# One passage of a transformer layer reordered: the last column group by token tile, units split by token tile, and a later gate product

## The chip, the cores and the metric

The kernel runs on one core of one Trainium2 chip. The metric is device time in microseconds, the median of three runs. One more execution was recorded by the hardware profiler; all durations, waits and orders in time below are from that one.

## The reference

One layer over 256 tokens of 2048 features, fp32, batch 1:

```python
u = _rms_norm(x, norm_mix_pre)
mix = hybrid_mixer(u, ...)      # proj = u @ w_in; three mixers; m = sum of gate * (y @ w_branch); m @ w_out
x = x + _rms_norm(mix, norm_mix_post)
hdn = jnp.square(jax.nn.relu(_rms_norm(x, norm_mlp_pre) @ w_mlp_up))
x = x + _rms_norm(hdn @ w_mlp_down, norm_mlp_post)
```

The mixers are a stick-breaking attention, a forgetting attention and RWKV-7 time mixing. RWKV's result is normed per head, gets a bonus, and is multiplied by a gate `g = sigmoid(gd) @ g_up`. `w_out` is 2048 x 2048, `w_mlp_up` 2048 x 8192.

## The kernel before, in words

**Number format and weights.** TensorE multiplies in a reduced fp32 format, so each fp32 operand is split in two: a rounded high part and the rest. Weights stream from HBM as tiles of 128 x 1024 (512 KB), `wraw` (L142), three buffers. `wsplit` (L148) makes a *pair* of one: ACT copies it, rounding, into `whi` (L151), DVE subtracts that from it into `wlo` (L152); three buffers of each. `wnext` (L155) hands out pairs and keeps `AHEAD` = 1 split in advance. `side` is a list of further loads, issued one by one behind weight loads.

**Activations.** `split` (L225) does the same to an activation of 256 tokens: high part by ACT (L232 with a scale), the rest by DVE (L233), side by side in one *pack* `pk` of 512 columns. `gemm` (L163) multiplies a weight pair with packs, feature-major: `whi` with all 512 columns (L167), `wlo` with the 256 of the high part (L171). `unit` (L177) or `up` (L1056) do two pairs to one PSUM bank `gps`. `tok` (L186) does it the other way round, token-major: for each of the two token tiles of 128 tokens, packs are stationary and 512 weight columns move. Each pair of weights is used for both token tiles at once (L213), but the last `lag` pairs are held, token tile 0 is done with them first (L197), and then token tile 1.

**Order of work.** PE's order up to the last column group of `w_out` is written by hand: the program issues in the order of the text (`written`, a manual schedule on PE), and small pieces of other work run as threads, generators that are resumed by `tick` (L124) when enough microseconds of matmuls, reckoned at 0.227 us each, have gone by. A thread's `yield 7.5` means: go on 7.5 us later by that clock. The other engines, and PE after `written` is closed, are put in order by a scheduler.

**RWKV's gate.** `gate_norm` (L743) is such a thread, run for each half `hf` of the heads. It norms the result, and for each of four head pairs multiplies by `ri` (DVE, L772), applies gain and bias (ACT, L773), adds the bonus (DVE, L774), loads the next pair's `gup` (two DMAs issued on ACT, L751 and L752), multiplies with PE (L778, L779; the *gate product*, into a PSUM bank `mps`, of which there are four) and multiplies the result in (DVE, L780).

**The passage.** Four column groups g of 512 columns of `m @ w_out` are done by `tok`. Each token tile's group gives a sum of squares (ACT, L968), and times the norm's gain goes to `mg` (DVE, L966). When the last group is there, `rstd_of` makes the factor (two operations of POOL, L938, L939), `add_mixed` (L955) adds factor times `mg` to `x1`, that is x + norm(mix). `turned` (L985) transposes `x1` (PE, L987) into `mps` banks, two k-tiles of both token tiles to a bank, and `split` makes the 16 packs `upk2`. For the last group `written` is closed and `lag` is 4. Then the MLP's units begin, each 16 x 512 columns (L167, L175) and 16 x 256 columns (L171). After a unit, `post` (L1069) squares its relu; for the first eight units it also takes the sum of squares of an eighth of `x1` (L1079). The first of the down-projection's weights go through six buffers of their own, `raw2` (L1043).

## Time and profile before

| | us |
|---|---|
| three runs | 1553.29, 1552.16, 1546.8 |
| median | 1552.16 |
| the profiled execution | 1552.68 |
| its span | 1550.9 |

Mean granted TensorE clock 0.997 of full speed. PE is busy 98% of the span, DVE 75%, ACT 58%, POOL 5%. The kernel reads 279.77 MB from HBM, 182 GB/s over the span.

How to read the rows: matmuls are recorded with start and length, and since they are pipelined the lengths overlap; the pitch is read between starts. A number in brackets is the time for which the engine waited before the instruction, with what released it. PE is matmul, PEld the weight load beside it. In a window's row the last three numbers are the granted clock, the share of DMA time, and GB/s.

### The profile page before, as it was taken

To read this page: it belongs to the slowest core of one execution; us is meant where nothing else is said; L and a number is where in the kernel's file an instruction comes from. 1 tells how busy PE (TensorE), PEld (TensorE's weight loads), DVE (VectorE), ACT (ScalarE), POOL (GpSimd) and SP (SyncE) were. 2 spreads that over 40 slices of the span, in tenths; PEclk is the share of its full clock that TensorE was granted. 3 is DMA by queue.
4 is the path that set the end of the run, shared out by engine and by line. 5 is a ranking of instruction groups with operands and counts; after the bars stand their busy time and mean duration, and the time that the engine had idled before them with its cause. 6 is when DMAs were issued, how large, how long until landed. Compare 5 with 4: busy or idle time off the path is not lost.

```text
span 1550.9 us, 22351 instructions
## 1 busy us (share of the span) xinstructions
PE 1515.4 (98%) x8318; PEld 1263.7 (81%) x8318; DVE 1157.1 (75%) x1554; ACT 891.9 (58%) x1326; POOL 84.0 (5%) x155
## 2 busy tenths in 40 slices
PE   7999999999999999999999999999999999999997
PEld 6888888888777788788886888878888887888885
DVE  6865567798548798457656768779988899788855
ACT  7664566554546544455445666667766676666542
POOL 0021000000000100000000000000000000000000
PEclk9999999999999999999999999999999999999999
DMA  7545455445534445435784557878888888887754
GB/s 258 190 165 173 151 184 171 167 152 190 167 121 146 165 160 192 152 134 180 252 285 135 199 186 207 249 219 246 261 248 253 252 239 228 268 241 225 220 194 136
DMA packets 101053, 308.49 MB, mean 199 GB/s; under 512 B 10065, under 2 KB 12497, under 8 KB 100817
## 3 DMA queue, kind: packets, MB, share of 16 engines
q1 hardware_dynamic: 90624, 278.56, 52.5%
q0 software_dynamic: 6912, 25.17, 8.8%
q10 hardware_dynamic: 3408, 3.34, 0.6%
q8 instruction: 65, 1.06, 0.3%
q14 instruction: 44, 0.35, 0.1%
HBM read 279.77 MB, written 2.10 MB: 182 GB/s over the span
## 4 chain that ended last, share of the span: by engine, by line
PE 28%; issue 12%; DMA 11%; DVE 4%; ACT 1%; POOL 0%; POOLq 0%; DVEq 0%; SPq 0%; ACTq 0%
PE gps L213 12%; DMA raw<-raw 7%; PE gps L167 6%; DMA raw<-in_wst_dram 5%; PE gps L171 3%; PE gps L197 3%; DVE wlo L152 2%; ACT whi L151 1%; PE mps L1149 1%; PE mps L1151 1%; PE mps L1150 1%; PE gps L1151 0%; PE gps L175 0%; PE gps L1149 0%; PE gps L1150 0%
## 5 line engine op out<-in xcount | busy, mean ns | idle before, releaser
L152 DVE TENSOR_TENSOR wlo<-raw,whi 128x1024 fp32r<-128x1024 f32 x590 | 715.9, 1222 | 256.5 <-ACT whi L151 238.2
L151 ACT ACTIVATE whi<-raw 128x1024 fp32r<-128x1024 f32 x590 | 618.8, 1056 | 336.8 <-PE gps L213 137.1
L167 PE MATMUL gps<-pk,whi 128*128 128x512 f32 x1495 | 380.3, 393 | 1.2 <-DVE tmp L1072 1.2
L167 PEld LDWEIGHTS gps<-pk,whi 128*128 128x128 f32 x1495 | 276.8, 188 | 58.7 <-issue 4.2
L213 PE MATMUL gps<-whi,pk 128*128 128x512 f32 x1144 | 291.2, 394 | 0.0
L213 PEld LDWEIGHTS gps<-whi,pk 128*128 128x128 f32 x1144 | 213.6, 188 | 45.7 <-issue 1.0
L171 PEld LDWEIGHTS gps<-pk,wlo 128*128 128x128 f32 x1599 | 218.3, 190 | 16.4 <-issue 1.2
L171 PE MATMUL gps<-pk,wlo 128*128 128x256 f32 x1599 | 224.4, 282 | 0.0
L213 PE MATMUL gps<-wlo,pk 128*128 128x512 f32 x572 | 157.4, 394 | 0.0
L213 PEld LDWEIGHTS gps<-wlo,pk 128*128 128x128 f32 x572 | 106.9, 188 | 23.2 <-issue 0.7
L1149 PE MATMUL mps<-whi,fm 128*128 128x512 f32 x192 | 76.2, 397 | 1.1 <-ACT whi L151 1.0
L1071 ACT ACTIVATE tmp<-gps 128x256 f32<-128x256 f32 x64 | 24.5, 383 | 90.7 <-PE gps L175 90.7
L1151 PE MATMUL mps<-wlo,fm 128*128 128x512 f32 x192 | 75.8, 395 | 0.9 <-DVE wlo L152 0.8
L1150 PE MATMUL mps<-whi,fm 128*128 128x512 f32 x192 | 75.1, 391 | 0.0
L1116 POOL DMA_DIRECT2D raw<-raw x48 | 41.9, 873 | 555.5 <-DVE raw L1113 347.5
L197 PE MATMUL gps<-whi,pk 128*128 128x512 f32 x264 | 72.0, 393 | 0.0
L1151 PE MATMUL gps<-wlo,fm 128*128 128x512 f32 x144 | 57.4, 399 | 2.1 <-DVE wlo L152 1.7
L1113 DVE TENSOR_TENSOR raw<-raw,raw 128x1024 f32<-128x1024 f32 x48 | 58.6, 1222 | 1.0
L1149 PE MATMUL gps<-whi,fm 128*128 128x512 f32 x144 | 56.9, 395 | 1.4 <-ACT whi L151 1.4
L197 PEld LDWEIGHTS gps<-whi,pk 128*128 128x128 f32 x264 | 49.3, 188 | 10.6 <-ACT whi L151 0.2
L1150 PE MATMUL gps<-whi,fm 128*128 128x512 f32 x144 | 56.4, 392 | 0.0
L213 PE MATMUL gps<-whi,fm 128*128 128x512 f32 x208 | 51.4, 389 | 0.0
(312 smaller groups left out, 1530.0 us busy)
## 6 DMA issues: line engine op xcount, KB each, us to landing
raw<-in_wst_dram SPq DMA_DIRECT2D x518, 512.0 KB, 4.3
raw<-raw POOLq DMA_DIRECT2D x48, 512.0 KB, 6.3
x<-in_x_dram SPq DMA_DIRECT2D x8, 256.0 KB, 5.5
...
```

What stands on the lines that cost most here:

```text
L151: A.activation(hi, raw, AF.Copy)
L152: V.tensor_tensor(lo, raw, hi.bitcast(F32), ALU.subtract)
L167: PE.matmul(ps, hi[:, i * 128:i * 128 + 128], pks[i], start=first and i == 0, stop=False)
L171: PE.matmul(ps[:, 0:T], lo[:, i * 128:i * 128 + 128], pks[i][:, 0:T], start=False, stop=False)
L197: PE.matmul(ps[tt], pks[k][:, c:c + 128], w[:, (k - k0) * 512:(k - k0) * 512 + 512], start=k == 0 and part == 0 and w is hl[0], stop=w is ...
L213: PE.matmul(ps[tt], pks[k][:, c:c + 128], w[:, (k - k0) * 512:(k - k0) * 512 + 512], start=k == 0 and part == 0 and w is hl[0], stop=False)
L1071: A.activation(b, ps[0][:, T:2 * T], AF.Copy)
L1113: V.tensor_tensor(R[a], R[a], R[b], ALU.add)
L1116: G.dma_start(out=R[a], in_=R[b], accum_op=ALU.add)
L1149: PE.matmul(Q[f], a, w, start=d == 0 and i == 0, stop=False)
L1150: PE.matmul(Q[f], b, w, start=False, stop=False)
L1151: PE.matmul(Q[f], a, wl, start=False, stop=d == 3 and i == 1)
```

## The change

Line numbers behind the first edit are 5 to 33 higher in the changed kernel; L157 there is L152 here, L218 is L213, L202 is L197, L777 to L785 are L772 to L780.

- **Gate product.** For the first half of the heads, `gate_norm` waits 11.5 in place of 7.5 before its four products and 2.8 in place of 2.0 between them.
- **Pairs.** From the first column group of `w_out` to the end of the passage, up to four pairs are split in advance. Three of four splits go to a pool `pa` with nine more buffers for each of `whi` and `wlo`, twelve in all.
- **Last column group.** `lag` is 8: token tile 0 is done with all eight pairs, then token tile 1. PE's order stays written.
- **Token tile 0.** Its x1 is added as before; a thread `turns0` puts its transposes between token tile 1's matmuls, four k-tiles of one token tile to a bank. Splits are of 128 columns, so there are 32 for 16.
- **Two units by token tile.** `share` does units 0 and 1 for one token tile and some k-tiles. Each k-tile costs a matmul of 2 x 128 columns with `whi` and one of 128 with `wlo`. Unit 0's share of tile 0 comes first, then the first transposes of tile 1, then unit 1's share of tile 0, then both units' share of tile 1 by fours.
- **Later.** x1 of tile 1 is added by eight operations of 256 columns with no transpose between. The eight squares of `x1` write to the unit's PSUM bank. `raw2`, `fm` and `sfm` move to a pool opened after `pa` is closed, so that the first six `raw2` loads are issued after the passage.

```diff
     def wsplit(raw):
-        hi = wpool.tile([128, HALF], F32R, tag="whi", name=nm("whi"), bufs=3)
-        lo = wpool.tile([128, HALF], F32R, tag="wlo", name=nm("wlo"), bufs=3)
+        turn[0] += 1
+        if more and turn[0] % 4:
+            hi, lo = (more[0].tile([128, HALF], F32R, tag=t, name=nm(t), bufs=9) for t in ("whi", "wlo"))
+        else:
+            hi, lo = (wpool.tile([128, HALF], F32R, tag=t, name=nm(t), bufs=3) for t in ("whi", "wlo"))
...
-        while len(wq) < 1 + AHEAD and (order or wpos[0] < wst.shape[0]):
+        while len(wq) < 1 + ahead[0] and (order or wpos[0] < wst.shape[0]):
...
-        yield 7.5
+        yield 7.5 if hf else 11.5
...
-            yield 2.0
+            yield 2.0 if hf else 2.8
...
-        return p2.tile([128, 7, 128], F32R, tag="fm", name=nm("fm"), bufs=16)
+        return p3[0].tile([128, 7, 128], F32R, tag="fm", name=nm("fm"), bufs=16)
...
+    more.append(pa)
+    ahead[0] = 4
...
+    upk2 = [pk() for _ in range(KT)]
+
+    def token_half(t, tt):
+        return t.rearrange("p (a t) -> p a t", a=2)[:, :, 128 * tt:128 * tt + 128]
+
+    def turned(k4, tt):
+
+        tr = mps()
+        for i in range(4):
+            PE.transpose(tr[:, 128 * i:128 * i + 128], x1[tt][:, (k4 + i) * 128:(k4 + i) * 128 + 128], C("ident"))
+        for i in range(4):
+            u = token_half(upk2[k4 + i], tt)
+            src = tr[:, 128 * i:128 * i + 128]
+            A.activation(u[:, 0], src, AF.Copy, scale=P("g3", k4 + i))
+            V.scalar_tensor_tensor(u[:, 1], src, P("g3", k4 + i), u[:, 0].bitcast(F32), ALU.mult, ALU.subtract)
+
+    def turns0():
+        for k4 in range(0, KT, 4):
+            yield 1.0 if k4 else 3.6
+            turned(k4, 0)
...
-        if g == 3:
-            assert not threads
-            written.close()
-        for tt, ps in enumerate(tok(mpk, 4 if g == 3 else 1)):
+        assert g < 3 or not threads
+        for tt, ps in enumerate(tok(mpk, 8 if g == 3 else 1)):
...
+            gained()
             if tt == 0:
-                gained()
                 for c in range(0, D, 512):
                     add_mixed(0, c, 512)
-            else:
-                pend = gained
+                start(turns0())
+
+    begun = []
+
+    def share(j, tt, ks):
+
+        if tt == 0 and ks[0] == 0:
+            begun.append((gps(), [wq.pop(0), wq.pop(0)]))
+        ps, hl = begun[j]
+        for k in ks:
+            hi, lo = (w[:, k % 8 * 128:k % 8 * 128 + 128] for w in hl[k // 8])
+            u = token_half(upk2[k], tt)
+            PE.matmul(token_half(ps, tt), hi, u, start=k == 0 and tt == 0, stop=False)
+            PE.matmul(ps[:, 128 * tt:128 * tt + 128], lo, u[:, 0], start=False, stop=k == KT - 1 and tt == 1)
+
+    assert len(wq) == 4 and not threads
+    for c in range(0, D, 256):
+        add_mixed(1, c, 256)
+    share(0, 0, range(KT))
+    turned(0, 1)
+    share(1, 0, range(0, 8))
+    turned(4, 1)
+    share(1, 0, range(8, KT))
+    for c in range(0, KT, 4):
+        if c < 8:
+            turned(c + 8, 1)
+        for j in range(2):
+            share(j, 1, range(c, c + 4))
+    written.close()
+    more.clear()
+    ahead[0] = AHEAD
+    pas.close()
...
-    for k2 in range(0, KT, 2):
-        while len(trs) < min(k2 // 2 + 4, 8):
-            trs.append(mps())
-            turned(2 * len(trs) - 2, 0)
-        if k2 == 8:
-            pend()
-        add_mixed(1, 128 * k2, 256)
-        turned(k2, 1)
-        for i in range(2):
-            u = pk()
-            split(trs[k2 // 2][:, i * T:i * T + T], u, P("g3", k2 + i))
-            upk2.append(u)
...
-        raw = p2.tile([128, HALF], F32, tag="raw2", name=nm("raw"), bufs=6)
+        raw = p3[0].tile([128, HALF], F32, tag="raw2", name=nm("raw"), bufs=6)
...
-                A.activation(junk(), x1[j % 2][:, 512 * (j // 2):512 * (j // 2) + 512], AF.Square,
+                A.activation(ps[0], x1[j % 2][:, 512 * (j // 2):512 * (j // 2) + 512], AF.Square,
...
+        if q == 0 and j < 2:
+            ps[0] = begun[j][0]
+            return [(None, lambda _: posts.append(post))]
```

On PE, in RWKV's first half, before (`gup` is the gate's weights, `wlo`, `whi` and `pk` are matmuls of `tok`, 566 and 568 the small low-rank products):

```order
L566 MATMUL mps_876_4614<-zx_1551,lor_838_4414 128x256
L568 MATMUL mps_877_4616<-zx_1551,lor_838_4414 128x256
L213 MATMUL gps_853_4484<-wlo_866_4556,pk_45_292 128x512
L778 MATMUL mps_885_4641<-zy_1605,gup_872_4596 128x256
L779 MATMUL mps_885_4641<-zz_879,gup_872_4596 128x256
L213 MATMUL gps_854_4485<-wlo_866_4556,pk_45_292 128x512
L213 MATMUL gps_853_4484<-whi_870_4587,pk_46_293 128x512 x2
L213 MATMUL gps_854_4485<-whi_870_4587,pk_46_293 128x512 x2
L213 MATMUL gps_853_4484<-whi_870_4587,pk_47_294 128x512 x2
L213 MATMUL gps_854_4485<-whi_870_4587,pk_47_294 128x512 x2
L778 MATMUL mps_889_4663<-zy_1605,gup_884_4637 128x256
```

and after, from the end of the second gate product to the third:

```order
L784 MATMUL mps_886_4647<-zz_879,gup_870_4592 128x256
L218 MATMUL gps_853_4484<-wlo_869_4577,pk_47_294 128x512
L218 MATMUL gps_854_4485<-wlo_869_4577,pk_47_294 128x512
L218 MATMUL gps_853_4484<-whi_883_4626,pk_48_295 128x512 x2
L218 MATMUL gps_854_4485<-whi_883_4626,pk_48_295 128x512 x2
L218 MATMUL gps_853_4484<-whi_883_4626,pk_49_296 128x512 x2
L218 MATMUL gps_854_4485<-whi_883_4626,pk_49_296 128x512 x2
L218 MATMUL gps_853_4484<-wlo_884_4627,pk_48_295 128x512
L218 MATMUL gps_854_4485<-wlo_884_4627,pk_48_295 128x512
L218 MATMUL gps_853_4484<-wlo_884_4627,pk_49_296 128x512
L783 MATMUL mps_895_4688<-zy_1605,gup_885_4643 128x256
L784 MATMUL mps_895_4688<-zz_879,gup_885_4643 128x256
```

Before, the third product (`mps_885`) follows the low-rank products by one matmul; after, the low-rank products are ahead of the second, and 13 matmuls stand between the second and the third.

On DVE at the same place, before (`g1` is RWKV's result, `b6` another RWKV operand):

```order
L558 TENSOR_SCALAR b6_837_4413<-b6_837_4413 128x512
L772 TENSOR_TENSOR g1_772_3976<-g1_772_3976,gn_841_4422 128x256
L559 TENSOR_TENSOR b6_837_4413<-b6_837_4413 128x512
L152 TENSOR_TENSOR wlo_871_4588<-raw_869_4585,whi_870_4587 128x1024
L774 TENSOR_TENSOR g1_772_3976<-g1_772_3976,g1_503_2610 128x256
L772 TENSOR_TENSOR g1_773_3977<-g1_773_3977,gn_841_4422 128x256
L780 TENSOR_TENSOR g1_772_3976<-mps_868_4570,g1_772_3976 128x256
```

and after:

```order
L563 TENSOR_SCALAR b6_837_4413<-b6_837_4413 128x512
L157 TENSOR_TENSOR wlo_869_4577<-raw_867_4574,whi_868_4576 128x1024
L564 TENSOR_TENSOR b6_837_4413<-b6_837_4413 128x512
L777 TENSOR_TENSOR g1_772_3976<-g1_772_3976,gn_841_4422 128x256
L157 TENSOR_TENSOR wlo_884_4627<-raw_882_4624,whi_883_4626 128x1024
L779 TENSOR_TENSOR g1_772_3976<-g1_772_3976,g1_503_2610 128x256
L777 TENSOR_TENSOR g1_773_3977<-g1_773_3977,gn_841_4422 128x256
L785 TENSOR_TENSOR g1_772_3976<-mps_871_4596,g1_772_3976 128x256
```

A second weight split, `wlo_884`, now stands between the first L772 (777) and the first product's L780 (785). The second L772 still stands just ahead of that.

On ACT there, before, and then after, up to the last DMA for the third product's weights (the first `gup` in the piece of after):

```order
L751 DMA gup_872_4596<-in_gup_dram 128x128
L752 DMA gup_872_4596<-in_gup_dram 32x128
L151 ACTIVATE whi_887_4648<-raw_886_4646 128x1024
L773 ACTIVATE g1_772_3976<-g1_772_3976,par_74 128x256
L751 DMA gup_884_4637<-in_gup_dram 128x128
L752 DMA gup_884_4637<-in_gup_dram 32x128
L151 ACTIVATE whi_895_4684<-raw_894_4682 128x1024
L773 ACTIVATE g1_773_3977<-g1_773_3977,par_74 128x256
```

```order
L756 DMA gup_885_4643<-in_gup_dram 128x128
L778 ACTIVATE g1_772_3976<-g1_772_3976,par_74 128x256
L580 ACTIVATE lw_877_4609<-mps_874_4603,wah_104 128x256
L581 ACTIVATE tha_879_4611<-mps_875_4605,wah_104 128x256
L582 ACTIVATE lw_877_4609<-lw_877_4609,cst_99 128x256
L778 ACTIVATE g1_773_3977<-g1_773_3977,par_74 128x256
L757 DMA gup_885_4643<-in_gup_dram 32x128
```

Before, both DMAs of a pair of heads stand together; after, the second DMA of `gup_885` is behind the second L773 (778).

In the passage, DVE before, from the addition of token tile 0 (`x1_1333`):

```order
L955 SCALAR_TENSOR_TENSOR x1_1333_7018<-mg_1335_7020,rs_1458_7646,x1_1333_7018 128x512 x4
L955 SCALAR_TENSOR_TENSOR x1_1334_7019<-mg_1336_7021,rs_1460_7680,x1_1334_7019 128x256 x4
L233 SCALAR_TENSOR_TENSOR pk_1465_7699<-mps_1461_7684,par_74,pk_1465_7699 128x256
L966 TENSOR_TENSOR mg_1336_7021<-gps_1432_7523,fm_1332_7017 128x512
L955 SCALAR_TENSOR_TENSOR x1_1334_7019<-mg_1336_7021,rs_1460_7680,x1_1334_7019 128x256
L233 SCALAR_TENSOR_TENSOR pk_1466_7702<-mps_1461_7684,par_74,pk_1466_7702 128x256
L233 SCALAR_TENSOR_TENSOR pk_1468_7711<-mps_1462_7687,par_74,pk_1468_7711 128x256
L955 SCALAR_TENSOR_TENSOR x1_1334_7019<-mg_1336_7021,rs_1460_7680,x1_1334_7019 128x256 x3
L233 SCALAR_TENSOR_TENSOR pk_1469_7714<-mps_1462_7687,par_74,pk_1469_7714 128x256
L233 SCALAR_TENSOR_TENSOR pk_1471_7723<-mps_1463_7690,par_74,pk_1471_7723 128x256
L152 TENSOR_TENSOR wlo_1487_7785<-raw_1485_7782,whi_1486_7784 128x1024
```

and after, from the second bank of token tile 0's splits to the last (`x1_1330` is token tile 1):

```order
L983 SCALAR_TENSOR_TENSOR pk_1346_7034<-mps_1480_7698,par_74,pk_1346_7034 128x128
L983 SCALAR_TENSOR_TENSOR pk_1347_7035<-mps_1481_7717,par_74,pk_1347_7035 128x128
L983 SCALAR_TENSOR_TENSOR pk_1348_7036<-mps_1481_7717,par_74,pk_1348_7036 128x128
L997 TENSOR_TENSOR mg_1332_7017<-gps_1453_7555,g2_1338_7026 128x512
L983 SCALAR_TENSOR_TENSOR pk_1349_7037<-mps_1481_7717,par_74,pk_1349_7037 128x128
L967 SCALAR_TENSOR_TENSOR x1_1330_7015<-mg_1332_7017,rs_1483_7762,x1_1330_7015 128x256 x2
L983 SCALAR_TENSOR_TENSOR pk_1350_7038<-mps_1481_7717,par_74,pk_1350_7038 128x128
L983 SCALAR_TENSOR_TENSOR pk_1351_7039<-mps_1482_7736,par_74,pk_1351_7039 128x128
L967 SCALAR_TENSOR_TENSOR x1_1330_7015<-mg_1332_7017,rs_1483_7762,x1_1330_7015 128x256 x2
L983 SCALAR_TENSOR_TENSOR pk_1352_7040<-mps_1482_7736,par_74,pk_1352_7040 128x128
L967 SCALAR_TENSOR_TENSOR x1_1330_7015<-mg_1332_7017,rs_1483_7762,x1_1330_7015 128x256 x2
L983 SCALAR_TENSOR_TENSOR pk_1353_7041<-mps_1482_7736,par_74,pk_1353_7041 128x128
```

Before, splits are of 256 columns and come after the additions of their columns; after, the additions of tile 1 stand between the last splits of tile 0.

PE in the passage, before, where the transposes turn into matmuls:

```order
L987 MATMUL mps_1461_7684<-ident_73,x1_1334_7019 128x128 x2
L987 MATMUL mps_1462_7687<-ident_73,x1_1334_7019 128x128 x2
L987 MATMUL mps_1463_7690<-ident_73,x1_1334_7019 128x128 x2
L987 MATMUL mps_1464_7693<-ident_73,x1_1334_7019 128x128 x2
L167 MATMUL gps_1488_7788<-pk_1465_7699,whi_1455_7634 128x512
L167 MATMUL gps_1495_7833<-pk_1465_7699,whi_1490_7807 128x512
L987 MATMUL mps_1467_7705<-ident_73,x1_1333_7018 128x128 x2
L987 MATMUL mps_1467_7705<-ident_73,x1_1334_7019 128x128 x2
L167 MATMUL gps_1488_7788<-pk_1466_7702,whi_1455_7634 128x512
```

and after, where unit 0's share of token tile 0 ends:

```order
L1022 MATMUL gps_1484_7774<-pk_1353_7041,whi_1470_7618 128x2x128
L1023 MATMUL gps_1484_7774<-pk_1353_7041,wlo_1471_7619 128x128
L1022 MATMUL gps_1484_7774<-pk_1354_7042,whi_1470_7618 128x2x128
L1023 MATMUL gps_1484_7774<-pk_1354_7042,wlo_1471_7619 128x128
L978 MATMUL mps_1485_7807<-ident_73,x1_1330_7015 128x128 x4
L1022 MATMUL gps_1486_7820<-pk_1339_7027,whi_1473_7630 128x2x128
L1023 MATMUL gps_1486_7820<-pk_1339_7027,wlo_1474_7631 128x128
L1022 MATMUL gps_1486_7820<-pk_1340_7028,whi_1473_7630 128x2x128
L1023 MATMUL gps_1486_7820<-pk_1340_7028,wlo_1474_7631 128x128
```

Before, PE has products of two units for each pack; after, all 32 products of unit 0's share of tile 0 stand ahead of tile 1's first transposes (`mps_1485`), and unit 1's (`gps_1486`) behind them.

27 lines of the change are left out of this document (14 added, 13 removed).

## The prediction

> **What bounds the kernel now.** I read the page first, for the shares.
>
> ```profile
> span 1550.9 us, 22351 instructions
> PE 1515.4 (98%) x8318; PEld 1263.7 (81%) x8318; DVE 1157.1 (75%) x1554; ACT 891.9 (58%) x1326; POOL 84.0 (5%) x155
> ```
>
> PE stands still for 1550.9 - 1515.4 = 35.5 us in all. A change that leaves the number of products alone can win a part of that, and what the clock loses, no more. So I asked next for PE's waits.
>
> ```profile
> PE gps L309 <- ACT whi L151: 8.8, 1, 8.8
> PE mps L987 <- DVE x L955: 2.1, 2, 1.8
> PE mps L987 <- DVE pk L233: 2.0, 4, 0.9
> PE mps L778 <- DVE g L780: 2.0, 1, 2.0
> ```
>
> The first is the start of the program. The next two are the passage to the MLP, the fourth is one wait in the gate product of RWKV. The change touches these two places. Third, the passage in the windows, each with the busy time of PE, PEld, DVE, ACT and POOL, then the granted clock:
>
> ```profile
> 800.00:820.00 20.00, 20.00 (x90) 16.57 (x89) 9.55 (x12) 8.62 (x11) 0.00 (x0) 1.00 0.67 226
> 840.00:860.00 20.00, 15.88 (x86) 11.50 (x85) 18.38 (x41) 15.21 (x38) 1.97 (x4) 1.00 0.32 108
> 860.00:880.00 20.00, 20.00 (x119) 17.76 (x118) 14.72 (x23) 13.97 (x26) 0.00 (x0) 1.00 0.60 198
> ```
>
> PE loses 4.12 us between 840 and 860, and there DVE works 18.38 of 20 us, ACT 15.21. So the passage is bound by DVE and ACT, which turn x1 into split packs. Fourth, PE's timeline through it (start, length, and in brackets the wait).
>
> ```profile
> 819.15 1.98 PE L213 MATMUL gps<-whi,pk 128*128 128x512 f32 x8
> ```
>
> ```profile
> 844.70 1.62 PE L987 MATMUL mps<-ident,x 128*128 128x128 f32 x8 [1.81 <-DVE x L955]
> ...
> 847.89 0.63 PE L987 MATMUL mps<-ident,x 128*128 128x128 f32 x4 [0.88 <-DVE pk L233]
> 848.28 1.17 PE L167 MATMUL gps<-pk,whi 128*128 128x512 f32 x4
> ...
> 854.41 1.12 PE L171 MATMUL gps<-pk,wlo 128*128 128x256 f32 x8
> 855.37 1.09 PE L167 MATMUL gps<-pk,whi 128*128 128x512 f32 x4
> ...
> 857.24 3.35 PE L167 MATMUL gps<-pk,whi 128*128 128x512 f32 x14
> 860.44 1.12 PE L171 MATMUL gps<-pk,wlo 128*128 128x256 f32 x8
> ...
> 862.79 0.40 PE L175 MATMUL gps<-pk,whi 128*128 128x512 f32 x1
> 863.03 1.09 PE L167 MATMUL gps<-pk,whi 128*128 128x512 f32 x4
> ```
>
> Call S = 819.15 the start of the last column group. Between starts, a 512-column matmul takes (860.44 - 857.24)/14 = 0.229 us, a 256-column one (855.37 - 854.41)/8 = 0.12, a transpose (848.28 - 847.89)/4 = 0.0975. The group's 96 matmuls end at about S+22.0. The first two units end at 863.03, but four products of the third unit lie ahead of that (0.92 us), so their own end is worth 862.1 = S+43.0. That is the number to beat. PE's work in it is 22.0 + 32 x 0.0975 + 2 x (32 x 0.229/2 + 16 x 0.12) = 36.3 us.
>
> Last, the stall in RWKV, with the clock in one slice behind it.
>
> ```profile
> 473.26 0.59 PE L778 MATMUL mps<-zy,gup 128*128 128x256 f32 x2
> ...
> 473.94 1.28 PE L213 MATMUL gps<-whi,pk 128*128 128x512 f32 x4
> ...
> 482.37 1.22 PE L778 MATMUL mps<-zy,gup 128*128 128x256 f32 x2 [1.99 <-DVE g L780]
> ...
> 483.89 0.99 PE L213 MATMUL gps<-wlo,pk 128*128 128x512 f32 x1
> 484.67 2.53 PE L213 MATMUL gps<-whi,pk 128*128 128x512 f32 x8
> 487.04 0.59 PE L778 MATMUL mps<-zy,gup 128*128 128x256 f32 x2
> ```
>
> ```profile
> 483.00:484.00 1.00, 1.00 (x5) 0.82 (x3) 1.00 (x2) 1.00 (x3) 0.00 (x0) 0.50 0.95 369
> ```
>
> From 482.37 to 487.04 PE takes 4.67 us for a gate product (0.68 us at 473.26) and nine matmuls (9 x 0.229 = 2.06), 2.74 us of work. The clock stands at half there. So this place costs 1.99 + 1.93 = 3.92 us, twice what the list of waits says.
>
> **The change: RWKV.** In the new order the first gate product stands 17 matmuls later, at 473.26 + 17 x 0.229 = 477.15. The second follows 13 matmuls and the four lora products later (an estimate: 4 x 0.12), at 477.15 + 0.68 + 2.98 + 0.48 = 481.3; the third, 13 matmuls on, at 484.95; the fourth at 488.6. The third waits for the first's PSUM buffer, which DVE's L780 frees.
>
> ```profile
> 481.91 0.41 DVE L780 TENSOR_TENSOR g<-mps,g 128x256 f32<-128x256 f32 x1
> ```
>
> ```profile
> L152 DVE TENSOR_TENSOR wlo<-raw,whi 128x1024 fp32r<-128x1024 f32 x12 | 14.7, 1222 | 11.7 <-ACT whi L151 10.6 <-PE gps L197 1.1
> ```
>
> DVE's order puts one weight split (1.22 us) more ahead of that L780. It slips from 481.91 to about 483.1, ends at 483.5, and PE asks only at 484.95: the wait goes, and with it the half clock. What is late next is the third product's weights. Of the two DMAs that bring them, the second now stands on ACT behind the second L773.
>
> ```profile
> 482.02 0.60 ACT L773 ACTIVATE g<-g,par 128x256 f32<-128x256 f32 x1 [0.20 <-DVE g L772]
> ```
>
> ```profile
> DMA to landing us min/median/max: 1.6/1.9/2.5
> ```
>
> That L773 needs the L772 that stands just ahead of the late L780 on DVE, so it runs from 483.1 to 483.7. The DMA lands 1.9 us later (1.6 to 2.5 here), at 485.6, a wait of 0.65 us (0.35 to 1.25); the fourth, by the same reckoning, waits 0 to 0.5. I take 0.7 for both. Term: -3.92 + 0.7 = **-3.2 us**, ends -3.9 and 0 (a new wait that again halves the clock).
>
> **The change: passage.** Two things are to hide the conversion of x1: token tile 0's matmuls all run first, so its half of x1 is ready early; and the first two units run per token tile. The price is that a split now covers 128 columns, four to a bank, 32 splits in place of 16. These rows price it:
>
> ```profile
> 853.09 0.87 DVE L233 SCALAR_TENSOR_TENSOR pk<-mps,par,pk 128x256 fp32r<-128x256 f32 x2
> ```
>
> ```profile
> 853.99 0.84 ACT L232 ACTIVATE pk<-mps,par 128x256 fp32r<-128x256 f32 x2 [1.08 <-DVE pk L233]
> ```
>
> DVE's pair ends at 853.09 + 0.87 = 853.96, and ACT's next copy begins 0.03 us later, having waited 1.08: within a bank, a copy waits until the subtraction before it has read. Only between banks do they overlap. So a bank of four costs four copies and three subtractions in series. Narrow durations:
>
> ```profile
> L739 ACT ACTIVATE g<-mps 128x64 f32<-128x64 f32 x32 | 4.6, 230 | 17.0 <-PE mps L728 12.3 <-PE mps L724 4.7
> L468 ACT ACTIVATE foxt<-foxt,foxsm 128x128 f32<-128x128 f32 x4 | 1.6, 388 | 0.0
> L457 DVE SCALAR_TENSOR_TENSOR foxt<-foxt,foxsm,con 128x128 f32<-128x128 f32 x4 | 1.4, 342 | 0.0
> L455 DVE SCALAR_TENSOR_TENSOR foxt<-mps,foxt 128x128 f32<-128x128 f32 x4 | 1.1, 286 | 2.2 <-PE mps L454 2.2
> ```
>
> A 128-column copy lies between 0.31 (a line from the 64-column 0.23 to the 256-column 0.47) and 0.388; I take 0.35. For the subtraction I take 0.342, the same operation, with 0.286 as the low end. A bank: 4 x 0.35 + 3 x (0.342 + 2 x 0.03) = 2.6 us (2.3 to 2.8). Sixteen splits: 4 x 2.6 + 0.4 = 10.8 us (9.5 to 11.4).
>
> Two more rows give the way from a sum of squares to the first addition into x1:
>
> ```profile
> 838.37 0.60 ACT L968 ACTIVATE junk<-gps 128x512 f32<-128x512 f32 x1 [0.73 <-PE gps L197]
> ```
>
> ```profile
> 840.69 2.74 DVE L955 SCALAR_TENSOR_TENSOR x<-mg,rs,x 128x512 f32<-128x512 f32 x4 [0.21 <-POOL rs L939]
> 844.15 1.67 DVE L955 SCALAR_TENSOR_TENSOR x<-mg,rs,x 128x256 f32<-128x256 f32 x4 [0.72 <-POOL rs L939]
> ```
>
> That is 840.69 - 838.37 = 2.32 us, and 2.74 for four additions of 512 columns. Tile 0's matmuls end at S+11.0, its x1 is whole at S+16.1. A weight split stands next on DVE, so the first subtraction comes at S+17.5. Ten of them, with one more weight split between, last until S+24.9. Tile 1's matmuls with the sixteen transposes inside end at S+22.0 + 1.6 = S+23.6. Its square waits on ACT for the tenth copy, to S+24.4; its additions can start at S+26.7. From here DVE alternates: eight additions of tile 1 (1.67 us for four) and the six subtractions left of tile 0. The sixteenth comes at about S+31.5. PE, which by the written order must end unit 0's whole share of tile 0 before anything else, does so at S+31.8. It had the work of ten packs by S+25.5, so it idles some 5 us there: as much as before, in another place.
>
> Then tile 1, whose first copy follows its transposes by 845.17 - 844.70 = 0.47 us:
>
> ```profile
> 845.17 0.47 ACT L232 ACTIVATE pk<-mps,par 128x256 fp32r<-128x256 f32 x1 [2.02 <-PE mps L987]
> ```
>
> After S+31.8 + 0.47 come 10.8 us of splits, to S+43.1, and then the last five packs' products (about 0.2 us each) to S+44.0. Tile 1's chain is the length of the old one's, since 32 narrow instructions cost DVE and ACT more than 16 wide ones. Term: 44.0 - 43.0 = **+1.0 us**. Ends: -1.3 from the quick bank, +0.6 from the slow one, +1 if the six late subtractions slip: -1 to +2.5.
>
> **Taken at nothing.** The narrow products: 64 of 256 columns at 0.12 and 64 of 128 columns, between half of 0.12 and the transposes' 0.0975, add 0.35 to 2.75 us to PE's work, covered by its idle time; uncovered they are the range's. The nine pairs split ahead: DVE and ACT have half of their time free at 800 to 820; the first copies into memory just freed may wait, 0 to +2. The eight squares of x1 moved into the up-projection: as long as L968's 0.60 each and a read of the sum, against 6 us free of 20 at 860 to 880. The six late weight loads: needed some 15 us after the passage, 0 to +1.
>
> **Sum.** -3.2 + 1.0 = -2.2 against the profiled execution's own 1552.68 us (its span of 1550.9 and 1.8 around it): 1550.5. The median of the three runs, 1552.16, lies 0.5 below that execution, inside their spread of 1546.8 to 1553.29.
>
> **Rivals.** *1, the cover holds.* If a copy need not wait for the subtraction in its bank, sixteen splits take 16 x 0.35 = 5.7 us. Tile 0 is done when tile 1's matmuls end and the passage comes down to PE's own 36.6 to 39: 38 gives -5.0 - 3.2 = -8.2, 1544.5. Against it stands the row with 1.08 us.
>
> *2, the sparse stretch halves the clock.* From S+25.5 to S+31.8 PE works perhaps a fifth of the time, and what follows, 16 transposes and 48 packs, is 11.2 us of work in 12.2. At half clock for 3.9 us, as after the stall at 480 (twice the 1.93 lost there), tile 1's splits wait for their transposes: up to +1.9, 1552.4. If the gaps between splits kept it low to the end, +11.2 less the 1.0 that was idle: 1550.5 + 10.2 = 1560.7. It decides from a gap of about 2 us, by the 1.99 above. For it: a gap of some 1.6 us (between the eleventh and the twelfth subtraction of tile 0, S+26.1 to S+27.9, less a pack) and four of 0.9 behind it. Against: 20 us of the passage before held 1.00 with a gap of 1.81. Middle: 1556.
>
> [...]
>
> *3, RWKV's wait only changes its name*, to the weights' DMA, long enough to halve the clock again: 1552.68 - 2.2 + 3.2 = 1553.7. It needs a landing over 3.2 us, for a wait of 2; the slowest here took 2.5.
>
> **Numbers.** My forecast 0.55, rival 1 0.15, rival 2 0.17, rival 3 0.13. A measurement of this kernel can tell about 0.5%, 7.8 us, from no change; only the better half of rival 1 and the far end of rival 2 reach that: faster 0.08, slower 0.04, same 0.88. The range goes from 1544.2 (rival 1) to 1556.5 (rival 2's middle), leaving out about 0.18.
>
> **What would show it.** Right: no wait at the third gate product over 1 us, and clock 1.00 there; after S+25 PE waits in small pieces for the subtractions of tile 0, DVE over 90% busy for 15 us; units done near S+44. Rival 1: copies following one another without a wait in a bank, units done before S+39. Rival 2: a granted clock of 0.5 behind S+25. I am wrong if PE idles less than 3 us in the passage, or if the gate product's wait is still there.

## The result, and the profile after

| | us |
|---|---|
| the change, median of 8 runs (1556.98 to 1564.47) | 1560.63 |
| before, 8 runs beside it (1543.95 to 1555.62) | 1550.04 |
| ratio, with its 95% interval | 1.0066 (1.0047 to 1.0084) |
| profiled execution of the change, its span | 1559.87, 1558.1 |

The change is slower by about 10 us, between 7 and 13. The forecast was no change that can be measured, 1550.5. The measured time lies above the whole range given, on the side that had a chance of 0.04.

The page's first lines, to be read against those of before:

```profile
span 1558.1 us, 22498 instructions
PE 1520.8 (98%) x8382; PEld 1271.8 (82%) x8382; DVE 1160.1 (74%) x1570; ACT 893.5 (57%) x1342; POOL 83.4 (5%) x155
```

The span grew by 7.2 us. PE's idle time hardly did: 1558.1 - 1520.8 = 37.3 us against 35.5. So most of the loss is PE's *busy* time, 5.4 us more, and no list of waits can show it. The waits of the two places that the change touches:

```profile
PE gps L1022 <- DVE pk L983: 3.0, 5, 0.8
...
PE mps L571 <- DVE SC L626: 1.4, 1, 1.4
PE mps L784 <- DMA gup<-in_gup_dram: 0.9, 1, 0.9
...
PE mps L978 <- DVE x L967: 0.8, 1, 0.8
```

The old waits (2.1 and 2.0 us in the passage, 2.0 in RWKV) are gone. In their place stand 3.8 us in the passage, in pieces of 0.8 at most, and 2.3 in RWKV. By this list the change costs nothing. The windows tell more. These are windows of the passage that begin and end with the stretch in which the clock was halved; after the length come PE, PEld, DVE, ACT and POOL, then the granted clock:

```profile
842.88:846.29 3.41, 2.96 (x24) 2.69 (x22) 2.75 (x6) 1.53 (x6) 0.66 (x2) 1.00 0.37 126
846.29:849.70 3.41, 1.60 (x8) 1.15 (x8) 3.35 (x11) 1.36 (x4) 0.16 (x1) 1.00 0.08 30
849.70:853.11 3.41, 2.70 (x12) 2.52 (x13) 1.35 (x6) 0.73 (x2) 0.00 (x0) 0.51 0.00 0
853.11:856.52 3.41, 3.41 (x19) 3.41 (x18) 1.39 (x4) 1.10 (x3) 0.00 (x0) 0.50 0.02 5
```

In the second row PE is busy 1.60 us of 3.41, 47%. In the next two the granted clock is one half, 6.83 us in all, and in the last of them PE is "100% busy". PE's timeline shows what that busy time is made of:

```profile
818.75 1.07 PE L202 MATMUL gps<-whi,pk 128*128 128x512 f32 x4
...
843.42 0.28 PE L1022 MATMUL gps<-pk,whi 128*128 128x256 f32 x1
...
843.60 0.34 PE L1022 MATMUL gps<-pk,whi 128*128 128x256 f32 x1
...
845.45 0.34 PE L1022 MATMUL gps<-pk,whi 128*128 128x256 f32 x1
...
846.49 0.39 PE L1022 MATMUL gps<-pk,whi 128*128 128x256 f32 x1 [0.64 <-DVE pk L983]
...
847.68 0.39 PE L1022 MATMUL gps<-pk,whi 128*128 128x256 f32 x1 [0.75 <-DVE pk L983]
...
851.09 0.58 PE L1022 MATMUL gps<-pk,whi 128*128 128x256 f32 x1 [0.36 <-DVE pk L983]
...
851.58 1.07 PE L978 MATMUL mps<-ident,x 128*128 128x128 f32 x4
...
855.76 1.00 PE L978 MATMUL mps<-ident,x 128*128 128x128 f32 x4
...
858.40 0.62 PE L978 MATMUL mps<-ident,x 128*128 128x128 f32 x4
...
866.60 2.08 PE L172 MATMUL gps<-pk,whi 128*128 128x512 f32 x8
```

S, the start of the last column group, is 818.75. Unit 0's share of token tile 0 ends at 851.58 = S+32.8, the first two units at 866.60 = S+47.9, where the profile of before has S+43.0. From 851.58 on PE never waits. Four transposes and eight packs take (855.76 - 851.58) = 4.18 us at half clock, and (858.40 - 855.76) = 2.64 where the clock comes back in between; the rows of the experiments below show 2.25 at full clock.

### The profile page after: what moved, and what is told of

It is laid out like the page before. It is cut to its first block, busy times and chain, and to the rows that moved or that the text cites. A ratio compares the mean times of both kernels' runs of the same rounds, so it can differ in the third digit from the quotient of the medians.

```text
span 1558.1 us, 22498 instructions
## 1 busy us (share of the span) xinstructions
PE 1520.8 (98%) x8382; PEld 1271.8 (82%) x8382; DVE 1160.1 (74%) x1570; ACT 893.5 (57%) x1342; POOL 83.4 (5%) x155
## 4 chain that ended last, share of the span: by engine, by line
PE 32%; DMA 8%; issue 8%; DVE 6%; ACT 2%; POOL 0%; POOLq 0%; DVEq 0%; ACTq 0%; SPq 0%
PE gps L172 8%; PE gps L218 8%; DMA raw<-in_wst_dram 5%; PE gps L176 5%; DVE wlo L157 3%; DMA raw<-raw 3%; PE gps L202 2%; ACT whi L156 2%; PE mps L1182 1%; PE mps L1184 1%; PE mps L1183 1%; PE gps L1184 1%; PE gps L1182 1%; PE gps L1183 1%; PE gps L1022 1%
## 5 line engine op out<-in xcount | busy, mean ns | idle before, releaser
L157 DVE TENSOR_TENSOR wlo<-raw,whi 128x1024 fp32r<-128x1024 f32 x590 | 715.4, 1222 | 254.7 <-ACT whi L156 236.9
L172 PE MATMUL gps<-pk,whi 128*128 128x512 f32 x1465 | 372.9, 393 | 2.5 <-DVE tmp L1102 2.5
L172 PEld LDWEIGHTS gps<-pk,whi 128*128 128x128 f32 x1465 | 271.9, 189 | 59.6 <-issue 5.9
L218 PE MATMUL gps<-whi,pk 128*128 128x512 f32 x1112 | 282.3, 393 | 0.0
L218 PEld LDWEIGHTS gps<-whi,pk 128*128 128x128 f32 x1112 | 207.0, 188 | 44.2 <-issue 1.0
L176 PEld LDWEIGHTS gps<-pk,wlo 128*128 128x128 f32 x1567 | 214.7, 191 | 16.2 <-issue 1.2
L176 PE MATMUL gps<-pk,wlo 128*128 128x256 f32 x1567 | 220.6, 283 | 0.0
L218 PE MATMUL gps<-wlo,pk 128*128 128x512 f32 x556 | 153.2, 394 | 0.0
L218 PEld LDWEIGHTS gps<-wlo,pk 128*128 128x128 f32 x556 | 103.7, 188 | 22.4 <-issue 0.7
L202 PE MATMUL gps<-whi,pk 128*128 128x512 f32 x296 | 81.1, 394 | 0.0
L1182 PE MATMUL mps<-whi,fm 128*128 128x512 f32 x192 | 76.3, 398 | 1.0 <-ACT whi L156 0.9
L1149 POOL DMA_DIRECT2D raw<-raw x48 | 41.9, 873 | 560.4 <-DVE raw L1146 376.9
L202 PEld LDWEIGHTS gps<-whi,pk 128*128 128x128 f32 x296 | 55.1, 188 | 11.4
L1182 PE MATMUL gps<-whi,fm 128*128 128x512 f32 x144 | 56.9, 395 | 1.5 <-ACT whi L156 1.4
L218 PE MATMUL gps<-whi,fm 128*128 128x512 f32 x208 | 51.4, 389 | 0.0
```

What stands on the lines that cost most here:

```text
L157: V.tensor_tensor(lo, raw, hi.bitcast(F32), ALU.subtract)
L172: PE.matmul(ps, hi[:, i * 128:i * 128 + 128], pks[i], start=first and i == 0, stop=False)
L176: PE.matmul(ps[:, 0:T], lo[:, i * 128:i * 128 + 128], pks[i][:, 0:T], start=False, stop=False)
L202: PE.matmul(ps[tt], pks[k][:, c:c + 128], w[:, (k - k0) * 512:(k - k0) * 512 + 512], start=k == 0 and part == 0 and w is hl[0], stop=w is ...
L218: PE.matmul(ps[tt], pks[k][:, c:c + 128], w[:, (k - k0) * 512:(k - k0) * 512 + 512], start=k == 0 and part == 0 and w is hl[0], stop=False)
L1149: G.dma_start(out=R[a], in_=R[b], accum_op=ALU.add)
```

## The experiments

Ratios are to the kernel before, on the same chip, with 95% intervals. Besides the time, three lengths of the profiled execution serve as measures: *RWKV* from the first matmul of L542 (L547 in the change), at 234.32 and 235.26 us, to S (584.83 before, 583.49 in the change); *passage* from S to the end of the first two units (42.96 and 47.85); and *down-projection* from the 49th matmul of L1149 (L1182 in the change), at 1012.25 and 1016.83 us, to the end of the span (538.6 and 541.2). Where an expectation says "to its last", the stretch ends with the last matmul of that line (439.5 before, 442.1 in the change).

### Each part alone

The kernel before with the two numbers of the gate product:

```diff
-        yield 7.5
+        yield 7.5 if hf else 11.5
...
-            yield 2.0
+            yield 2.0 if hf else 2.8
```

> The kernel before with the gate product's two numbers alone (11.5 and 2.8 for 7.5 and 2.0 in the first half of the heads). Theory A (the gate edit saves the stall of 2.0 us and its half clock of 1.9 us, and gets back about 2.3 us as two new waits, for the third product's weights and for the PSUM bank after it): 1 to 2 us faster than before, no change that a measurement can tell, and the new waits of 0.9 and 1.4 us in its profile. Theory B (the new waits come only with the rest of the change): 3 to 4 us faster. Neither makes it slower.

Measured: 0.9996 (0.9983 to 1.0009). RWKV is 582.25, so 2.6 us shorter; the passage is 43.1. The place where the clock stood at half:

```profile
482.00:488.00 6.00, 5.87 (x27) 4.60 (x26) 6.00 (x12) 4.06 (x10) 1.77 (x4) 1.00 0.72 249
```

The change with the old two numbers:

```diff
-        yield 7.5 if hf else 11.5
+        yield 7.5
...
-            yield 2.0 if hf else 2.8
+            yield 2.0
```

> The changed kernel with the gate product's two numbers put back. Theory A (the passage loses 5 us, and nothing behind it is slower because of the change): 4 to 7 us slower than before, the two units done 47 to 48 us after the last column group starts, half clock for two stretches of 3.4 us there. Theory B (half of the loss is behind the passage, from the moved pools, squares and loads): 9 to 13 us slower, with the stage from 900 to 1500 longer by 4 us or more.

Measured: 1.0076 (1.0054 to 1.0099); RWKV 584.82, passage 47.0. The whole loss is there without the new gate numbers, so it comes with the passage's part of the change. The gate product's new place is a gain of 2.6 us in its own stretch, which the time does not show. This profile again has a half clock of 6.83 us in the passage, from 848.7, the old one at 483.4, and one of 3.41 us at 1224.

### Is it the half clock?

The change with two 512-column matmuls of no use (their result is not read) ahead of each of the last six packs of unit 0's share of tile 0, so that PE has work in its gaps:

```diff
         for k in ks:
...
+            if (j, tt) == (0, 0) and k >= 10:
+                fill(hl[0][0])
```

> The changed kernel with twelve extra matmuls of 512 columns (2.75 us of work whose result nobody reads), two ahead of each of the last six packs of unit 0's share of token tile 0, where PE waits for subtractions. Theory A (the idle stretch halves the clock, and that costs about 3 us): clock 1.00 through the passage, units done at S+44.5 to 45.5 for S+47.85, and 2 to 4 us faster than the change in spite of more work. Theory B (the subtractions set the end, the clock only slows what waits anyway): units done at S+47 to 48 still, no change in time.

Measured: 1.0028 (1.0013 to 1.0043). Windows and timeline of this kernel:

```profile
844.00:848.00 4.00, 3.64 (x19) 2.55 (x19) 3.94 (x13) 1.65 (x5) 0.14 (x1) 1.00 0.04 15
848.00:852.00 4.00, 3.91 (x33) 3.47 (x32) 1.74 (x6) 1.18 (x4) 0.00 (x0) 1.00 0.01 4
```

```profile
849.07 0.62 PE L978 MATMUL mps<-ident,x 128*128 128x128 f32 x4
...
851.32 0.61 PE L978 MATMUL mps<-ident,x 128*128 128x128 f32 x4
...
861.94 1.85 PE L172 MATMUL gps<-pk,whi 128*128 128x512 f32 x7
```

No half clock. Four transposes and eight packs take 851.32 - 849.07 = 2.25 us, and from tile 1's first transposes to the end of the two units it is 861.94 - 849.07 = 12.9 us, where the change takes 15.0. So adding work to PE made the kernel faster, and the half clock costs 2.1 us in this stretch. Between the ratios lie 5.9 us, with an interval of about 2.2 to 9.6 (from the two intervals, as independent): the traced 2.1 is at its low end. The units end at S+46.3, between what the two theories gave: 1.6 earlier than in the change, because tile 0's share ends 0.6 later (PE waits 1.6 there for x1, where the change waits 0.8). The two profiles' spans differ by 7.5 us. Of that, 3.1 lie before S (RWKV 581.84 here, 583.49 there, and a half clock at 177 us in the profile of the change, on which more below) and 2.8 in the down-projection, where the two kernels are alike. So the gain in time is not the clock's alone.

### Why PE had gaps

The second question is why tile 0's packs came so late. The prediction has the copy of ACT wait for DVE's subtraction in the same PSUM bank. This kernel is the change with `turned` issuing the four copies of a bank first and then its four subtractions:

```diff
         for i in range(4):
             u = token_half(upk2[k4 + i], tt)
+            A.activation(u[:, 0], tr[:, 128 * i:128 * i + 128], AF.Copy, scale=P("g3", k4 + i))
+        for i in range(4):
+            u = token_half(upk2[k4 + i], tt)
             src = tr[:, 128 * i:128 * i + 128]
-            A.activation(u[:, 0], src, AF.Copy, scale=P("g3", k4 + i))
```

> The changed kernel with the splits of a bank issued as four copies and then four subtractions, in place of copy and subtraction in turn. Theory A (in a bank each copy waits for the subtraction before it; in this order ACT works on one bank while DVE works on the other): sixteen splits in 6.5 to 7.5 us, token tile 0 done before tile 1's additions, units done at S+39 to S+41.5, clock 1.00, 6 to 8 us faster than the change and 1 to 5 faster than before. Theory B (DVE's and ACT's own durations set the chain): units done at S+44 or later, 0 to 3 us faster than the change.

Measured: 0.9998 (0.998 to 1.0017), and a second time:

> The kernel of the fourth experiment once more. Its passage and gate product end 4.5 us earlier than before's. If the down-projection is not touched by them: 3 to 6 us faster than before. If the down-projection gives it back, as it seemed there: no change, and the down-projection from its 48th group to its last 437 us or more, where the kernels with the passage of before took 433.8 to 439.5.

0.9986 (0.9972 to 1.0). DVE's timeline in the change, tile 1's second bank and the start of the third:

```profile
857.21 0.35 DVE L983 SCALAR_TENSOR_TENSOR pk<-mps,par,pk 128x128 fp32r<-128x128 f32 x1 [1.40 <-ACT pk L982]
857.99 0.35 DVE L983 SCALAR_TENSOR_TENSOR pk<-mps,par,pk 128x128 fp32r<-128x128 f32 x1 [0.43 <-ACT pk L982]
858.78 0.35 DVE L983 SCALAR_TENSOR_TENSOR pk<-mps,par,pk 128x128 fp32r<-128x128 f32 x1 [0.44 <-ACT pk L982]
859.56 0.61 DVE L983 SCALAR_TENSOR_TENSOR pk<-mps,par,pk 128x128 fp32r<-128x128 f32 x2 [0.43 <-ACT pk L982]
860.60 0.35 DVE L983 SCALAR_TENSOR_TENSOR pk<-mps,par,pk 128x128 fp32r<-128x128 f32 x1 [0.43 <-ACT pk L982]
```

One of ACT's copies there, which waits for DVE in its turn:

```profile
857.59 0.37 ACT L982 ACTIVATE pk<-mps,par 128x128 fp32r<-128x128 f32 x1 [0.42 <-DVE pk L983]
```

And with the copies first, where each row is a whole bank:

```profile
834.49 1.12 DVE L985 SCALAR_TENSOR_TENSOR pk<-mps,par,pk 128x128 fp32r<-128x128 f32 x4
836.13 1.13 DVE L985 SCALAR_TENSOR_TENSOR pk<-mps,par,pk 128x128 fp32r<-128x128 f32 x4 [0.52 <-ACT pk L981]
837.96 1.13 DVE L985 SCALAR_TENSOR_TENSOR pk<-mps,par,pk 128x128 fp32r<-128x128 f32 x4 [0.70 <-ACT pk L981]
...
840.14 1.12 DVE L985 SCALAR_TENSOR_TENSOR pk<-mps,par,pk 128x128 fp32r<-128x128 f32 x4
```

Within a bank a split every 0.79 us becomes one every 0.28; what is left between the banks is DVE's wait for ACT's copies, which in turn wait 0.69 for PE's transposes. Tile 0's splits end at 841.3, before tile 1's additions begin. PE:

```profile
817.53 1.07 PE L202 MATMUL gps<-whi,pk 128*128 128x512 f32 x4
...
844.83 0.62 PE L978 MATMUL mps<-ident,x 128*128 128x128 f32 x4
...
857.54 1.83 PE L172 MATMUL gps<-pk,whi 128*128 128x512 f32 x7
```

```profile
844.00:848.00 4.00, 4.00 (x39) 4.00 (x37) 3.56 (x11) 1.40 (x5) 0.00 (x0) 1.00 0.02 4
```

Unit 0's share of tile 0 ends at 844.83 = S+27.3 (S+32.8 in the change, of which 0.8 is the wait for x1), PE is never idle, the clock stays whole, and tile 1 takes 857.54 - 844.83 = 12.7 us. The passage is 40.0, 7.8 shorter than in the change: 5.5 up to the end of tile 0's share, 2.3 behind it with the clock. In the second profile, where PE waits 1.0 for x1, it is 41.2. By the quotient of the two ratios it takes 0.993 of the change's time (0.990 to 0.996, the intervals taken as independent). Against the kernel before it is level.

Since tile 1 is then PE's own work, narrow matmuls count. One more kernel, copies first and unit 1 not split by token tile (512 and 256 columns again, after tile 1's transposes):

```diff
     share(0, 0, range(KT))
     turned(0, 1)
-    share(1, 0, range(0, 8))
     turned(4, 1)
-    share(1, 0, range(8, KT))
...
-        for j in range(2):
-            share(j, 1, range(c, c + 4))
+        share(0, 1, range(c, c + 4))
+        whole(range(c, c + 4))
```

> The kernel of the fourth experiment (copies first) with unit 1 no longer done by token tile: once token tile 1's splits come, each pack is used for both of unit 0's narrow matmuls and for unit 1's matmuls of 512 and 256 columns. Theory A (with the splits out of the way, the passage is bound by PE, and a pack of two narrow matmuls costs 0.231 us where half of 0.229 + 0.12 would be 0.175): PE's work shrinks by 16 x (0.462 - 0.349) = 1.8 us, units done 1 to 2.5 us earlier than in the fourth experiment, at S+38 to S+39.5, time 1 to 3 us below it and 2 to 5 below before. Theory B (the cover was needed): PE waits after unit 0's share of tile 0, units done no earlier than in the fourth experiment.

Measured: 0.9991 (0.9974 to 1.0007), passage 39.5. Half a microsecond better in the profile, not to be told from the last one by the time.

### Where the rest of the loss is

By the profiles, the two units end 4.5 us later in the change than before, and 4.6 earlier with the copies first. By the ratios, the ends of the programs are 10 us later and level. So some microseconds are lost behind the passage too. What the change alters there was tried piece by piece. First the kernel before with the MLP's buffers in a pool opened after the passage, as in the change; its six `raw2` loads early or, in the second kernel, held until the last pack:

```diff
-        raw = p2.tile([128, HALF], F32, tag="raw2", name=nm("raw"), bufs=6)
+        raw = p3[0].tile([128, HALF], F32, tag="raw2", name=nm("raw"), bufs=6)
```

and in the second one also

```diff
+    hold = pa.tile([128, 18432], F32, tag="hold", name="hold", bufs=1)
+    G.tensor_scalar(hold[:, 0:1], upk2[KT - 1][:, T:T + 1].bitcast(F32), 1.0, None, ALU.mult)
     pas.close()
```

> The kernel before with its buffers laid out as in the change (x1 and mg first, the down-projection's fm, sfm and raw2 in a pool opened behind the passage), the passage itself untouched; the six raw2 loads are issued 19 weight loads later than before. Theory A (what the change loses beyond the passage is no matter of the buffers): no change, within 2 us. Theory B (the other places or the later loads slow the down-projection): 2 to 5 us slower, all of it behind 1000.

> As the one before, and a one-column operation on POOL at the end of the passage holds the six raw2 loads back until then, as in the change. Theory A: no change, within 2 us. Theory B: 2 to 5 us slower, by as much as the one before or more.

Measured: 0.9999 (0.9984 to 1.0015) and 1.0011 (0.9994 to 1.0027). The moved pools and the late loads are not it. With them ran the change and the kernel before again, as controls:

> The changed kernel as it is, once more beside the kernel before. If its loss is the same in every run: 8 to 12 us slower again, units done at S+47 to 48 with two stretches of half clock, and the down-projection from its 48th group to its last some 442 us or more, for 439.5 in the profile before. If half of the loss was the luck of these runs: 4 to 6 us slower and a down-projection of 437 to 440.

> The kernel before, once more, measured against itself: no change within 2 us. Its profile tells how far the stages differ from one execution to another: the passage and the up-projection within 0.5 us, the gate product's wait 2 us with or without the half clock behind it, the down-projection within 5 us.

Measured: 1.0064 (1.0039 to 1.009) and 0.9999 (0.9982 to 1.0016). The first repeats the loss, and in its profile the 6.83 us of half clock, from 849.6. The profile of the second holds a surprise, an old-order passage with a half clock:

```profile
841.10:844.50 3.40, 1.62 (x10) 0.84 (x8) 2.67 (x5) 2.20 (x5) 1.40 (x2) 1.00 0.40 145
844.50:847.90 3.40, 2.99 (x10) 1.84 (x10) 3.19 (x8) 2.33 (x8) 0.00 (x0) 0.50 0.00 0
```

In the first profile of the same kernel the stretch of 3.41 us with the least work, counted in steps of 3.4133 us from the start of its half clock at 482.36, has more of it; the clock stayed whole (what the profiles show of this is told under the hardware):

```profile
840.76:844.17 3.41, 1.82 (x11) 0.98 (x9) 2.69 (x5) 2.24 (x5) 1.40 (x2) 1.00 0.41 154
```

The passage with the half clock is 43.2 all the same, against 43.0: PE's waits for splits in it are 1.6 us (L987 for `pk`), where they are 2.0 in the first profile. In the old order PE has waits behind that stretch too (0.88 at 847.89 and 0.41 at 849.87 in the first profile); in the change it never waits from 851.58 on.

The nine more pairs with the old passage:

```diff
+        if more and turn[0] % 4 and wpos[0] <= mlp:
+            hi, lo = (more[0].tile([128, HALF], F32R, tag=t, name=nm(t), bufs=9) for t in ("whi", "wlo"))
```

> The kernel with the pools moved (fifth experiment) and now with nine more pairs and four split in advance during the out-projection, but the passage as before. Theory A (pairs and buffers are no part of the loss): within 2 us of before. Theory B (the loss behind the passage comes with the pairs): 3 to 5 us slower, all of it behind 1000.

Measured: 1.0005 (0.999 to 1.002); the passage is 41.4, 1.6 shorter, but not the time. Then two kernels with copies first and one more thing put back: the three `whi` and `wlo` buffers turn in their old order behind the passage, and the squares of `x1` write to `junk` again:

```diff
-            hi, lo = (wpool.tile([128, HALF], F32R, tag=t, name=nm(t), bufs=3) for t in ("whi", "wlo"))
+            ring[0] += 1
+            hi, lo = (wpool.tile([128, HALF], F32R, tag=f"{t}{ring[0] % 3}", name=nm(t), bufs=1) for t in ("whi", "wlo"))
```

> The kernel of the fourth experiment with the three weight buffers of each kind taken strictly in turn (0, 1, 2), as in the kernel before; in the changed kernel and its variants the nine more pairs leave them in the turn 0, 2, 1 behind the passage. Theory A (the buffers' turn slows the down-projection by some 4 us): 3 to 5 us faster than the fourth experiment's kernel, 4 to 5 below before, the down-projection from its 48th group to its last 434 to 437 us. Theory B (it has nothing to do with it): as the fourth experiment, 0 to 2 us below before.

```diff
-                A.activation(ps[0], x1[j % 2][:, 512 * (j // 2):512 * (j // 2) + 512], AF.Square,
+                A.activation(junk(), x1[j % 2][:, 512 * (j // 2):512 * (j // 2) + 512], AF.Square,
```

> The kernel of the fourth experiment with the eight squares of x1 written to their own buffers in SBUF again, in place of the unit's PSUM bank. Theory A (the moved squares have a part in what is lost behind the passage): 2 to 5 us faster than the fourth experiment's kernel. Theory B: no change against it, 0 to 2 us below before.

Measured: 0.9994 (0.9979 to 1.0009) and 0.9987 (0.9973 to 1.0002). Their passages are 40.0 and 40.9, their down-projections 540.9 and 537.2. Neither buys back what the traces of the passage promise. Last, two kernels that ask whether more instructions, or their place in the program, cost something later. The kernel before with 64 matmuls of 128 columns in its passage, eight in each step of the loop (results not read):

```diff
             upk2.append(u)
+        for _ in range(8):
+            PE.matmul(spare[:, 0:128], mpk[KT - 1][:, 0:128], mpk[KT - 1][:, 0:128], start=True, stop=True)
```

> The kernel before with 64 more matmuls of 128 columns on PE in the passage (their result is not read), as many more as the change has, so that all PE code behind them lies as far back as in the change; the first units then start behind the last transposes, so the passage is some 5 to 8 us longer. Theory A (where the code lies slows the down-projection): from the 48th group to the end 540 us or more, for 536 in the kernels with the passage of before, and 4 us more in the time than the passage explains. Theory B: no change there.

Measured: 1.0108 (1.0091 to 1.0126). It does not answer its question, since its passage grew to 54.8 us and its first units came in another order; what happened there is told under the hardware. And the kernel before with 64 small matmuls at the start of the program:

```diff
+    z, zp = tmp(), mps()
+    G.memset(z, 0.0)
+    for i in range(64):
+        PE.matmul(zp[:, 0:32], z[:, 0:128], z[:, 0:32], start=True, stop=True)
```

> The kernel before with 64 small matmuls of 32 columns on zeros at the very start of PE's program, where PE waits some 9 us for the first weights; everything behind them is the same, in the same order, only 64 matmuls later in PE's code. Theory A (where the code lies slows the down-projection): 3 to 5 us slower, all behind 1000, from the 48th group of the down-projection to the end 539 us or more. Theory B (the place of the code has no part in it): no change within 2 us.

Measured: 1.0114 (1.0083 to 1.0145). All of the 18 us is at the start, where the 64 calls are 128 matmuls in the trace and last 27.5 us; the down-projection is 532.9, so the instructions' place in the program is not it.

Over all profiles the down-projection takes 532.9 to 539.5 us with the old passage (mean 536.3 of eight profiles) and 537.0 to 545.6 with the new one (mean 539.7 of nine), a difference of 3.4 with a standard error of 1.3. The 545.6 alone has a half clock inside, the one at 1224; without it the difference is 2.7. Between the kernel before and the change themselves it is 2.6 in the first pair of profiles and 0.4 in the second. One place where it may arise: ACT's copies of weights that wait for the accumulating transfers which prepare them. This is ACT's row of these copies, before and after (from 1012 us to 1545):

```profile
L151 ACT ACTIVATE whi<-raw 128x1024 fp32r<-128x1024 f32 x256 | 266.5, 1054 | 108.5 <-DMA raw<-raw 31.7 <-PE gps L213 27.8 <-PE gps L1150 16.1
```

```profile
L156 ACT ACTIVATE whi<-raw 128x1024 fp32r<-128x1024 f32 x258 | 268.4, 1054 | 114.5 <-DMA raw<-raw 38.4 <-PE gps L218 26.4 <-PE gps L1183 14.4
```

The wait on `raw<-raw` is 31.7 us before and 38.4 after, though every engine has the same instructions in the same order there. But in the second profiles of the same two kernels it is 36.8 before and 30.5 after, and over all profiles 20.3 to 36.8 with the old passage and 27.4 to 39.0 with the new one. So it is not shown that the new passage, 150 us earlier, makes these transfers later. Whether it lengthens the down-projection, and how, stays **open**: the pools, the late loads, the pairs, the turn of the buffers, the squares and the place of the code were tried, and none explains it.

## Why the prediction was wrong

**The step that failed** is the sum of the passage, +1.0 us. It measured +4.9 in the change's profile, +3.9 in the second one and +4.1 with the passage alone, against 42.96. Three things make it up, with the numbers of the first profile:

- *Tile 0's share*, forecast to end at S+31.8, ended at S+32.8. The chain was right: splits are in series within a bank, and a bank of four takes 860.60 - 857.99 = 2.61 us from its second split to the next one's, 2.6 as priced. Not foreseen was the wait of 0.8 for x1 ahead of tile 0's first transposes (L978 in the list of waits): it moves the end of tile 1's matmuls from S+23.6 to 843.42 = S+24.7, and what hangs on it. In the second profile that wait is not there, and the share ends at S+31.8, as forecast.
- *Tile 1 is bound by PE, not by its splits.* The prediction priced a pack's products at about 0.2 us, called them covered, and let the chain of splits set the end, 12.2 us after the share. A pack takes (845.45 - 843.60)/8 = 0.231, and 48 of them with 16 transposes of 0.0975 are 12.6 us; with a whole clock the stretch measured 12.9 and 12.7. This is +0.7, and it is why nothing covered the next. The term that was mis-sized stands under "Taken at nothing": the narrow products were to add 0.35 to 2.75 us to PE's work, covered. Their 64 packs take 64 x 0.231 = 14.8 us where the wide products took 11.2, so they add 3.6, most of it where PE has no idle time.
- *The clock was halved.* Rival 2 came as it was told, a sparse stretch (1.60 us of work in 3.41) and then half clock (6.83 us), and about at its near price: "up to +1.9", measured 2.1. Its chance, 0.17, and the point from which it decides were wrong. The text set that at a gap of about 2 us; none here is over 0.75. The argument against it, that the old passage kept 1.00 with a gap of 1.81, came from one profile: of the seven profiles whose passage has the old order and no matmuls added, three have a half clock there, and their passages are no longer (43.0 to 43.2) than those without (43.0 to 43.1; 41.4 with the nine pairs). Ahead of the half clock PE had 1.60 us of work in 3.41 in the change and 1.62 in 3.40 in the second profile of before; with 1.82 in 3.41 the clock stayed whole in the first. An estimate from the timeline of before, which takes 1.62 us as little enough: laid through that passage in steps of 3.41 us, one stretch has no more work than that for some 0.57 of all places at which the steps can begin. So the chance of a half clock was about one half in the old order already (three of seven measured). That rival 2's far end, 1560.7, is nearly the measured 1560.63 is luck: the clock did not stay low to the end, and the passage accounts for 4.9 us of the loss.

1.0 + 0.7 + 2.1 is 3.8 of the 3.9 by which the change's profile misses the term.

**RWKV**, forecast -3.2: the gate product's old wait and the half clock behind it went, as forecast, and the new wait came with the name and the size given (0.9 for `gup`; 0.65 taken, 0.35 to 1.25 given). It is in four of the nine profiles with the new numbers, 0.2 to 0.9 us:

```profile
482.66 0.59 PE L783 MATMUL mps<-zy,gup 128*128 128x256 f32 x2
...
486.53 0.59 PE L783 MATMUL mps<-zy,gup 128*128 128x256 f32 x2
488.00 0.67 PE L784 MATMUL mps<-zz,gup 128*128 128x256 f32 x2 [0.88 <-DMA gup<-in_gup_dram]
```

Product and weights both come later than worked out (486.53 for 484.95), in part because this profile runs 0.9 us late by then. What the sum lacked is the wait at 502 us for the next step of RWKV's state, 1.4 us (`SC` in the list of waits; 0.2 to 1.5 in the kernels with the new numbers, absent with the old). The stretch is 584.7 to 584.9 in seven of the eight profiles with the old numbers, 582.4 in the mean of nine with the new (581.5 to 583.5): -2.4, and -1.3 and -2.1 in the change's own two. The eighth old one, 583.2, is the only one of the eight with no half clock behind the wait: the 1.93 us that the prediction read from one slice is seen there as 1.6. Rival 3 did not come.

**Rival 1** came in no kernel as written: a copy does wait for the subtraction in its bank (0.42 us above), and its passage would have been 38. With the order of issue turned it nearly came, 40.0.

**Taken at nothing**: the nine pairs are worth -1.6 in the passage's profile with the old order; the late loads and squares, nothing. The down-projection was not in the sum at all; it is longer by 3.4 in the means, with the doubts given above. (The range's lower end, 1544.2, is not the 1544.5 that the text works out for rival 1; nothing hangs on it.)

**The signs given.** Fulfilled: no wait over 1 us at the third product, clock 1.00 there, small waits for the subtractions of tile 0. Failed: DVE over 90% busy for 15 us (it is 8.84 of 13.64 us in the four windows above), units done near S+44. Rival 2's sign, a clock of 0.5 behind S+25, came at S+31.

**What doesn't add up.** RWKV -2.4, passage +4.3 (mean of the three profiles) and down-projection +3.4 make +5.3; the measured time shows +7 to +13. Some 2 to 8 us of the loss are not accounted for. In the first pair of profiles nothing is missing: the 7.2 us between the spans are +0.9 ahead of the RWKV stretch, -1.3 in it, +4.9 in the passage, +0.1 between it and the down-projection, and +2.6 there. But the median of the runs moved by 10.6. The change's profile has a half clock of 3.41 us at 177 us, where the kernels do the same work, and no run shows that the change has a part in that. The rest is below what two or three profiles can tell, since the times of one kernel differ by 7 to 12 us.
